# A hybrid Conformer and mLSTM backbone on one core: the scheduler's default state against a timeline of every engine

## The chip, the core and the metric

One Trainium2 chip, one of its cores. A core has five engines with a queue of instructions each: TensorE (PE, matrix products into PSUM), VectorE (DVE) and ScalarE (ACT) for elementwise work, GpSimd (POOL), and SyncE (SP), which here only issues DMAs from HBM to SBUF. Each engine takes its queue in order, and an instruction waits on semaphores for those of other engines. The metric is the device time in microseconds (us) of one launch: the median of several runs.

## The reference

Two layers over 256 latent and 256 context tokens of width 1024, in float32. Layer 0 mixes tokens with a Conformer convolution, layer 1 with a bidirectional chunkwise mLSTM of 4 heads; after each comes a squared-ReLU MLP of width 4096. Every part is modulated by adaLN (shift, scale and gate from a condition vector) and followed by a layer norm:

```python
def adaln(cvec, w, b):
    return jnp.split(jax.nn.silu(cvec) @ w + b, 6, axis=-1)

def modulate(x, shift, scale):
    return x * (1 + scale) + shift

def conformer_conv(u, rows, w_pw1, b_pw1, w_dw, b_dw, ln_g, ln_b, w_pw2, b_pw2):
    a = u @ w_pw1 + b_pw1
    a = a[..., :CONV_DIM] * jax.nn.sigmoid(a[..., CONV_DIM:])
    ...
    a = jax.nn.silu(layer_norm(a + b_dw, ln_g, ln_b))
    return a @ w_pw2 + b_pw2
```

The sub-layer is `x <- LN(ALPHA*x + gate * F(modulate(x)))`; the output is the latent stream, 256 x 1024.

## The kernel before

**Products.** A float32 product is made of three products of a faster type. `split` (L150, L151) makes of a tile a rounded high half (ACT casts `wh`) and the rest as a low half (DVE subtracts, `wl`); `mm3` (L181, L184, L185) adds hi·hi, hi·lo and lo·hi in PSUM. `mm3t` (L212 to L214) does the same with the operands exchanged, `mm_any` (L196, L197) with a right side that holds both halves. Weights come in tiles `raw` of 1 MB, of which there are three buffers, all loaded on SP (`raw_load`, L144); a tile `raw` is split into two pairs `wh`, `wl` of 1024 columns, of which there are four each. The PSUM tags are mm (3 banks), ln (2), fl (1) and cv (2).

**The start** (L607 to L664). The first modulation and the first pointwise product of the Conformer run in eight stages f = 0 to 7, each over 128 of the 1024 features. `start0(f)` loads three things on SP: `raw` with the adaLN weights (1 MB), `x` (256 KB, L622) and `F` with pointwise weights (256 KB, L624); then `ada_mm` (L343) makes the modulation of these features on PE, and DVE copies it (L630). `start1(f)` splits `F` into wh, wl, folds the modulation on PE (L351), makes shift and scale on DVE (L637, L638), and `affine_split` makes the modulated tile `u` with its halves: ACT the high half (L600), DVE the product again (L601) and the low half by subtraction (L603). `start2` multiplies: 4 output tiles by 3 matmuls. They are written so that the L343 of stage f+1 goes ahead of the products of stage f:

```python
    for f in range(DT):
        start2(f, (0,))
        if f + 1 < DT:
            start1(f + 1)
        start2(f, (1, 2, 3))
        if f + 2 < DT:
            start0(f + 2)
    pin[0] = False
    later = tc.high_priority(-100)
    later.__enter__()
```

**Behind it** lies a block of lower priority (L669 to L741) that builds tables of cosines for the convolution by DFT: DVE steps L696 to L713 on a tile `tab`, loads of `bdw` and of two tiles `L` with the taps, and `taps` (L739), two matmuls per half. Then the rest of the pointwise product with weights `pw1`, the transform, and the later layers follow. `ada_mm` also makes the later modulations, of which `fl_136_759` is the next.

**What sets the order.** The code is written in Python, and the framework's scheduler turns it into one queue per engine. It may take an instruction ahead of others where no data and no buffer forbid it, and places it by priority and by its own picture of when engines and data are ready. The code binds it in three ways: `tc.issue_after(i)` puts what is issued in it behind instruction i, `tc.keep_in_program_order` pins a matmul among others that are pinned (only while `pin[0]` holds, in the start), and `tc.high_priority(-100)` makes a block less urgent. Nothing pins the loads, ACT or DVE in the start beyond that. The scheduler also gives out the buffers in that order, so which earlier use a load waits for depends on it, and it spreads the semaphores of the DMAs of SP and ACT over eight: from the ninth DMA on an issue waits for the landing of an earlier one.

## Time and profile before

| | us |
|---|---|
| median of 3 runs | 1661.2 |
| lowest, highest | 1659.6, 1662.05 |
| span of the profiled execution | 1658.8 |
| PE busy in it | 1647.3 |
| DVE busy | 1042.7 |
| ACT busy | 730.4 |

The page gives for each engine its busy time and share of the span, then the chain of work that ended last, followed back from the last instruction, in shares of the span by engine. The view of waits lists, for an engine, line and releaser, the idle time in total, how often, and the longest. A row of the timeline has the start, the length, the engine, the line, the operation, out<-in, partitions and elements, how many instructions it joins, and in brackets the idle time before it with what ended it. "SPq" is an issue of a DMA on SP, which says nothing yet of its landing; the first reader's wait shows that. A matmul of 512 columns starts about 0.23 us behind the one before, though its row says 0.39: they overlap. The table over stretches gives for a window its length, then busy time and count of PE, PEld (weight loads), DVE, ACT and POOL, the clock granted to TensorE, the busy share of the DMA engines and GB/s.

### The profile page before, as it was taken

The page shows a single profiled execution, that of the slowest core. Times are in us where ns is not written, and L with a number is a line of the kernel's source. Part 1 is how long each engine was busy: PE and PEld are TensorE (multiplying, and loading weights), DVE is VectorE, ACT ScalarE, POOL GpSimd, SP SyncE. Part 2 cuts the span into 40 slices and gives each one's busy share as a digit, 9 for nine tenths or more (in the row PEclk, how much of TensorE's full clock was granted, in tenths as well). Part 3 has the DMA queues.
Part 4 walks back from the last instruction along what each step waited for, and adds up shares of the span by engine and source line. Part 5 has one row for each costly group of instructions (what it writes and reads, how often), then busy time and mean ns, then how long its engine had stood idle before and what let it go on. Part 6 is the DMA issues. An engine that isn't in the chain of part 4 may idle for free.

```text
span 1658.8 us, 22681 instructions
## 1 busy us (share of the span) xinstructions
PE 1647.3 (99%) x8824; PEld 1357.0 (82%) x8824; DVE 1042.7 (63%) x1875; ACT 730.4 (44%) x1174; POOL 14.3 (1%) x64
## 2 busy tenths in 40 slices
PE   9999999999999999999999999999999999999998
PEld 7665998888888998877787899888878888878887
DVE  6564895666535776762254753563489776776677
ACT  4313572232324475652133533442478654555453
POOL 0000000000000000000000000000000000000001
PEclk9999999999999999999999999999999999999999
DMA  9666223434424066557774852554466655675552
GB/s 359 229 213 239 96 71 116 163 123 147 137 102 153 1 225 204 184 194 272 282 255 145 301 179 80 178 190 151 147 227 219 212 211 202 242 283 186 178 186 93
DMA packets 80411, 305.80 MB, mean 184 GB/s; under 512 B 11854, under 2 KB 30066, under 8 KB 50352
## 3 DMA queue, kind: packets, MB, share of 16 engines
q1 hardware_dynamic: 57840, 288.06, 49.5%
q10 hardware_dynamic: 22464, 16.30, 3.0%
q8 instruction: 69, 1.13, 0.3%
q14 instruction: 38, 0.31, 0.1%
HBM read 286.47 MB, written 17.86 MB: 183 GB/s over the span
## 4 chain that ended last, share of the span: by engine, by line
PE 93%; DVE 4%; DMA 1%; ACT 1%; issue 1%; SPq 0%; DVEq 0%; ACTq 0%
PE mm L181 17%; PE mm L184 17%; PE mm L185 17%; PE mm L196 7%; PE mm L197 4%; PE mm L212 3%; PE mm L214 3%; PE mm L213 3%; PE cv L212 2%; PE fl L343 1%; PE cv L214 1%; PE cv L213 1%; DVE wl L151 1%; PE ln L181 1%; PE cv L878 1%; PE ln L184 1%
## 5 line engine op out<-in xcount | busy, mean ns | idle before, releaser
L151 DVE TENSOR_TENSOR wl<-raw,wh 128x1024 fp32r<-128x1024 f32 x344 | 418.5, 1221 | 248.1 <-ACT wh L150 246.5
L150 ACT CAST wh<-raw 128x1024 fp32r<-128x1024 f32 x344 | 358.6, 1051 | 463.3 <-PE mm L184 245.1
L184 PE MATMUL mm<-u,wh 128*128 128x512 f32 (+1 forms) x808 | 292.2, 362 | 0.2 <-DVE u L603 0.2
L181 PE MATMUL mm<-u,wh 128*128 128x512 f32 (+1 forms) x680 | 244.1, 360 | 0.0
L185 PE MATMUL mm<-u,wl 128*128 128x512 f32 (+1 forms) x680 | 241.5, 356 | 0.0
L184 PEld LDWEIGHTS mm<-u,wh 128*128 128x128 f32 x808 | 153.0, 189 | 23.3 <-issue 1.0
L181 PEld LDWEIGHTS mm<-u,wh 128*128 128x128 f32 x680 | 128.8, 190 | 24.9 <-issue 6.3
L185 PEld LDWEIGHTS mm<-u,wl 128*128 128x128 f32 x680 | 128.8, 190 | 17.9
L212 PE MATMUL mm<-wh,xl 128*128 128x512 f32 x256 | 101.2, 395 | 0.9 <-ACT wh L150 0.8
L181 PE MATMUL mm<-xm,wh 128*128 128x512 f32 x256 | 101.0, 395 | 0.0
L213 PE MATMUL mm<-wh,xl 128*128 128x512 f32 x256 | 100.0, 391 | 0.0
L185 PE MATMUL mm<-xm,wl 128*128 128x512 f32 x256 | 99.7, 389 | 0.0
L214 PE MATMUL mm<-wl,xl 128*128 128x512 f32 x256 | 99.4, 392 | 0.1
L181 PE MATMUL mm<-hid,wh 128*128 128x512 f32 (+1 forms) x256 | 93.3, 364 | 0.0
L185 PE MATMUL mm<-hid,wl 128*128 128x512 f32 (+1 forms) x256 | 92.8, 363 | 0.0
L184 PE MATMUL mm<-hid,wh 128*128 128x512 f32 (+1 forms) x256 | 92.8, 363 | 0.0
L196 PE MATMUL mm<-x,wh 128*128 128x512 f32 x232 | 81.1, 398 | 0.0
L184 PE MATMUL mm<-qq,wh 128*128 128x272 f32 x256 | 73.9, 289 | 0.0
L181 PE MATMUL mm<-qq,wh 128*128 128x272 f32 x256 | 73.5, 288 | 0.0
L185 PE MATMUL mm<-qq,wl 128*128 128x272 f32 x256 | 73.5, 288 | 0.0
L196 PE MATMUL mm<-u,wh 128*128 128x512 f32 x192 | 68.6, 399 | 0.0
L1120 DVE SCALAR_TENSOR_TENSOR x<-mm,ada,x 128x256 f32<-128x256 f32 x64 | 28.5, 479 | 62.4 <-PE mm L185 62.4
(537 smaller groups left out, 3245.2 us busy)
## 6 DMA issues: line engine op xcount, KB each, us to landing
raw<-w SPq DMA_DIRECT2D x64, 1024.0 KB, 4.8
raw<-wo SPq DMA_DIRECT2D x32, 1024.0 KB, 5.3
raw<-ada_w SPq DMA_DIRECT2D x22, 1024.0 KB, 7.3
ar<-ada_w SPq DMA_DIRECT2D x80, 256.0 KB, 4.1
raw<-wv SPq DMA_DIRECT2D x16, 1024.0 KB, 7.3
raw<-wqT SPq DMA_DIRECT2D x16, 1024.0 KB, 5.6
raw<-wq SPq DMA_DIRECT2D x16, 1024.0 KB, 6.2
raw<-wk SPq DMA_DIRECT2D x16, 1024.0 KB, 4.8
```

Source lines behind the costliest of these rows:

```text
L150: c = nc.scalar.copy(hi, src)
L151: lastsub[0] = nc.vector.tensor_tensor(lo, src, hi.bitcast(F32), op=ALU.subtract).ins
L181: a = nc.tensor.matmul(ps, wh, xh, start=start, stop=False)
L184: nc.tensor.matmul(ps, wh, xl, start=False, stop=False)
L185: lastmm[0] = nc.tensor.matmul(ps, wl, xh, start=False, stop=stop).ins
L196: todo = [lambda s_, e_: nc.tensor.matmul(ps, wh, r[0], start=s_, stop=e_), lambda s_, e_: nc.tensor.matmul(ps[:, :n], wl, r[0][:, :n], st ...
L197: lambda s_, e_: nc.tensor.matmul(ps[:, :n], wl, r[0][:, :n], start=s_, stop=e_)]
L212: nc.tensor.matmul(ps, xh, wh, start=start, stop=False)
L213: nc.tensor.matmul(ps, xl, wh, start=False, stop=False)
L214: nc.tensor.matmul(ps, xh, wl, start=False, stop=stop)
L343: a = mark_unit[0] = nc.tensor.matmul(ps[32 * j:32 * j + 32], cs[:, kt, 14 - 2 * v:46 - 2 * v], blocks[kt], start=first and kt < 4, stop=l ...
L1120: nc.vector.scalar_tensor_tensor(res[m][:, sl_], p_, g[:, m:m + 1], res[m][:, sl_], op0=ALU.mult, op1=ALU.add)
```

## The change

One argument where the scheduler is set up:

```diff
-    with _tile.TileContext(nc) as tc:
+    with _tile.TileContext(nc, schedule_with_timeline_sim=True) as tc:
         hybrid_kernel(tc, *args, o)
```

The scheduler now keeps a simulated timeline of every engine while it orders the program, and places by that. `hybrid_kernel` is the same text: the same loads, matmuls and elementwise steps, and two loads of ACT's function tables fewer (26 for 28). What differs is the order on each engine, and with it the buffers and the waits. PE has 2526 lines of difference among some 8150, DVE 1857, ACT 1067, SP 246, POOL 30. PE's order in the first seven stages of the start is the same. Three places, in which the numbers of tiles are those of the program (`F_19_171` is stage 1's F, `F_30_217` stage 2's, `F_85_447` stage 7's; `u_91_472` and `u_92_473` are the halves of stage 7's u):

On SP, in the start, from stage 1's x on (`raw_29_214` is stage 2's raw, `x_28_213` to `x_83_443` are the x of stages 2 to 7):

```order
 L622 DMA x_17_167<-xT 128x512
-L624 DMA F_19_171<-pw1a 128x512
 L144 DMA raw_29_214<-ada0_w 128x2048
 L622 DMA x_28_213<-xT 128x512
+L622 DMA x_39_259<-xT 128x512
+L622 DMA x_50_305<-xT 128x512
+L622 DMA x_61_351<-xT 128x512
+L622 DMA x_72_397<-xT 128x512
+L622 DMA x_83_443<-xT 128x512
+L624 DMA F_19_171<-pw1a 128x512
```

Stage 1's F, before the third load behind stage 1's raw, is now the ninth: all x and the next raw go first. Right behind it on SP, in the same way, up to stage 2's F (`raw_40_260` and `raw_51_306` are the raw of stages 3 and 4, `bdw` and the two `L` belong to the block of tables):

```order
+L144 DMA raw_40_260<-ada0_w 128x2048
+L728 DMA bdw_570<-wdw_d 128x1024
+L733 DMA L_99_574<-wdw_d 31x512
+L733 DMA L_100_575<-wdw_d 31x512
+L144 DMA raw_51_306<-ada0_w 128x2048
 L624 DMA F_30_217<-pw1a 128x512
```

Two raw of later stages and the loads of the tables now go ahead of it.

Before stage 7, first SP again (`raw_115_614` and `raw_125_683` are weights pw1 for the products behind the start, `raw_134_755` adaLN weights for `fl_136_759`):

```order
 L624 DMA F_74_401<-pw1a 128x512
-L144 DMA raw_84_444<-ada0_w 128x2048
-L622 DMA x_83_443<-xT 128x512
-L624 DMA F_85_447<-pw1a 128x512
-L144 DMA raw_101_579<-wg_d 128x256
 L144 DMA raw_115_614<-pw1 128x2048
 L144 DMA raw_125_683<-pw1 128x2048
+L624 DMA F_85_447<-pw1a 128x512
 L144 DMA raw_134_755<-ada_w 128x2048
```

Stage 7's F now stands behind the two raw of pw1. On DVE there, from the stage's scale to the low half of its u, before:

```order
L638 TENSOR_SCALAR sc1p_109<-ln_90_467,vecs_72 128x2
L699 TENSOR_SCALAR tab_524<-F_94_509,pc_510 128x128
L601 TENSOR_SCALAR S_93_474<-x_83_443,sc1p_109,sh1p_110 128x256 x2
L700 TENSOR_SCALAR tab_524<-F_94_509,pc_510 128x128
L701 TENSOR_SCALAR tab_524<-tab_524 128x63
L603 TENSOR_TENSOR u_92_473<-S_93_474,u_91_472 128x512
```

and now:

```order
L638 TENSOR_SCALAR sc1p_109<-ln_90_467,vecs_72 128x2
L706 TENSOR_TENSOR tab_524<-tab_524,F_95_531 128x384
L151 TENSOR_TENSOR wl_117_617<-raw_115_614,wh_116_616 128x1024
L601 TENSOR_SCALAR S_93_474<-x_83_443,sc1p_109,sh1p_110 128x256 x2
L707 SCALAR_TENSOR_TENSOR F_95_531<-tab_524 128x384
L151 TENSOR_TENSOR wl_120_647<-raw_115_614,wh_119_646 128x1024
L151 TENSOR_TENSOR wl_127_686<-raw_125_683,wh_126_685 128x1024
L708 TENSOR_SCALAR tab_524<-F_95_531 128x384
L603 TENSOR_TENSOR u_92_473<-S_93_474,u_91_472 128x512
```

Three of the four small steps are done earlier; three subtractions of whole weight tiles and three wider steps of the tables stand between now. ACT has the three casts that belong to them ahead of its half of `u`.

On PE, between stage 6 and stage 7 (`cv_4_108` is stage 6's last product, `mm_1_105` stage 7's first; `fl_136_759` stood about 120 matmuls later, behind the products with pw1):

```order
 L184 MATMUL cv_4_108<-u_81_427,wh_77_417 128x512
 L185 MATMUL cv_4_108<-u_80_426,wl_78_418 128x512
+L343 MATMUL fl_136_759<-raw_134_755,cs_91 32x512 x4
 L181 MATMUL mm_1_105<-u_91_472,wh_88_463 128x512
 L184 MATMUL mm_1_105<-u_92_473,wh_88_463 128x512
```

The first half of the next modulation, four matmuls with their raw, has come ahead of stage 7.

## The prediction

> **What bounds the kernel now.** First the page: busy times, then the chain of work that ended last.
>
> ```profile
> PE 1647.3 (99%) x8824; PEld 1357.0 (82%) x8824; DVE 1042.7 (63%) x1875; ACT 730.4 (44%) x1174; POOL 14.3 (1%) x64
> ...
> PE 93%; DVE 4%; DMA 1%; ACT 1%; issue 1%; SPq 0%; DVEq 0%; ACTq 0%
> ```
>
> TensorE is busy in 99% of a span of 1658.8 us, and 93% of the chain is its own. So I ask first how much an order could win, by the view of waits, on PE:
>
> ```profile
> PE cv L175 <- DVE ones L129: 1.1, 1, 1.1
> PE mm L212 <- ACT wh L150: 0.8, 1, 0.8
> PE ln L739 <- DVE tab L713: 0.5, 1, 0.5
> PE fl L343 <- DMA raw<-ada_w: 0.3, 1, 0.3
> PE cv L878 <- DVE F L867: 0.3, 1, 0.3
> PE mm L184 <- DVE u L603: 0.2, 1, 0.2
> PE ln L549 <- DVE ln L537: 0.2, 1, 0.2
> ```
>
> All of PE's waits together are 3.4 us, 1.1 of them the program's first. The one other loss is the clock: full in all 40 slices of the page, but by a table over stretches
>
> ```profile
> 41.90:63.60 21.70, 21.21 (x81) 16.20 (x82) 17.98 (x34) 8.66 (x11) 1.99 (x8) 0.93 0.72 238
> ```
>
> it was 0.93 over these 21.7 us, which is 1.5 us lost. With the same matmuls an order can win at most some 4 us (3.4 - 1.1 + 1.5). It can lose wherever a producer with little to spare is put later, and the start is such a place: there each of eight stages needs three loads that have just come.
>
> **The loads of stages 1 and 2.** Before, SP issues for each stage raw (1 MB of 1024 KB), x and F (256 KB each). Now five further x stand ahead of stage 1's F, and raw, bdw, two L and another raw ahead of stage 2's. PE's order in stages 0 to 6 is pinned and stays. What a place in the queue costs is read from ACT's timeline, where the cast of stages 1 to 4 starts when its F lands, and from two issues on SP:
>
> ```profile
> 11.44 0.62 ACT L150 CAST wh<-F 128x512 fp32r<-128x512 f32 x1 [0.97 <-DMA F<-pw1a]
> 15.18 0.62 ACT L150 CAST wh<-F 128x512 fp32r<-128x512 f32 x1 [0.73 <-DMA F<-pw1a]
> 20.28 0.62 ACT L150 CAST wh<-F 128x512 fp32r<-128x512 f32 x1 [1.76 <-DMA F<-pw1a]
> 24.03 0.62 ACT L150 CAST wh<-F 128x512 fp32r<-128x512 f32 x1 [1.02 <-DMA F<-pw1a]
> ```
>
> ```profile
> 3.84 0.66 SPq L624 DMA_DIRECT2D F<-pw1a  x1
> ...
> 33.42 4.73 SPq L144 DMA_DIRECT2D raw<-pw  x2
> ```
>
> The F issued at 3.84 lands at 15.18: 11.3 us for 256 KB, so it waits for what was issued ahead of it. From 11.44 to 24.03 three stages of 1.5 MB came in 12.6 us, 0.36 MB per us; the best of them took 3.74 us, 0.40. I take 0.38. Now PE's rows at the places concerned, and the end of DVE's work for a stage:
>
> ```profile
> 10.29 1.07 PE L343 MATMUL fl<-raw,cs 128*32 128x256 f32 x16 [0.29 <-DMA raw<-ada_w]
> ...
> 16.03 0.40 PE L184 MATMUL mm<-u,wh 128*128 128x512 f32 x1
> ...
> 20.43 0.40 PE L184 MATMUL mm<-u,wh 128*128 128x512 f32 x1
> ...
> 32.28 1.07 PE L343 MATMUL fl<-raw,cs 128*32 128x256 f32 x16
> ...
> 36.69 1.07 PE L343 MATMUL fl<-raw,cs 128*32 128x256 f32 x16
> ...
> 41.92 0.50 PE L184 MATMUL mm<-u,wh 128*128 128x512 f32 x1 [0.23 <-DVE u L603]
> ```
>
> ```profile
> 23.05 0.69 DVE L603 TENSOR_TENSOR u<-S,u 128x512 fp32r<-128x512 f32 x1 [0.39 <-ACT u L600]
> ```
>
> Stage 1's raw has landed by 10.2 (PE waited for it until 10.29). Behind it now come x, raw, six x and F: 0.25 + 1 + 1.5 + 0.25 = 3.0 MB, or 7.9 us: F at 18.1 (17.7 to 18.5 by the two rates) instead of 11.4. From a landed F to the low half of u it is 23.74 - 20.28 = 3.5 us, so stage 1's second matmul goes from 16.03 to 21.6: 5.5 us late. Behind that F stand 1 + 0.5 + 0.12 + 1 + 0.25 = 2.87 MB, 7.6 us: stage 2's F at 25.7, its u at 29.2, against 20.43: **8.7 us late** (7.9 to 9.5). The 5.5 are contained in it. Stages 3 to 6 have one raw and one F each to wait for, 3.3 us against 4.4 us of PE work per stage, and their x are there: nothing more.
>
> **Stage 7.** Three edits meet. On SP its F stands behind two raw of pw1. The first row of SP above shows what these wait for: the issue at 33.42 follows the end of PE's L343 of 32.28 (33.35), the second, at 37.8, that of 36.69 (37.76): a slot of the three raw buffers. The second raw now takes the slot that the L343 of 32.28 frees, so it is issued at 33.35 + 8.7 = 42.0 and F at 42.4. How long that takes is on the page:
>
> ```profile
> raw<-w SPq DMA_DIRECT2D x64, 1024.0 KB, 4.8
> ...
> ar<-ada_w SPq DMA_DIRECT2D x80, 256.0 KB, 4.1
> ```
>
> raw lands at 46.8, F 0.25 / 0.38 = 0.7 later: 47.5 (46.5 if it needs only 4.1; 50 if the raw ahead still fills the queue). Then DVE. Between the stage's scales and the subtraction L603 that makes u stand, instead of four small steps, L706 to L708 of the tables and three subtractions of whole weight tiles, and ACT has three casts ahead of its half of u. Their lengths in DVE's timeline:
>
> ```profile
> 39.07 0.68 DVE L151 TENSOR_TENSOR wl<-F,wh 128x512 fp32r<-128x512 f32 x1
> ...
> 40.12 0.73 DVE L601 TENSOR_SCALAR S<-x,sc1p,sh1p 128x256 f32<-128x256 f32 x2
> ...
> 41.17 0.69 DVE L603 TENSOR_TENSOR u<-S,u 128x512 fp32r<-128x512 f32 x1
> ...
> 42.57 0.56 DVE L706 TENSOR_TENSOR tab<-tab,F 128x384 f32<-128x384 f32 x1
> ...
> 44.18 0.55 DVE L707 SCALAR_TENSOR_TENSOR F<-tab 128x384 f32<-128x384 f32 x1
> 44.76 0.36 DVE L708 TENSOR_SCALAR tab<-F 128x384 f32<-128x384 f32 x1
> ...
> 47.58 3.46 DVE L151 TENSOR_TENSOR wl<-raw,wh 128x1024 fp32r<-128x1024 f32 x3
> ```
>
> Cast of F 0.62, then 0.68 + 0.56 + 3.46 + 0.73 + 0.55 + 0.36 + 0.69 = 7.0 on DVE: 7.6 us, all needed in a row. u is ready at 55.1, against PE's 41.92, where it had nothing to spare (it waited 0.23): PE is **13.2 us late** (12 to 16), the 8.7 included. Third, four matmuls of L343 for the next modulation, 32 us early on PE, stand ahead of stage 7. Their raw waits for the slot that the L343 of 36.69 frees, is issued at 46.5 and lands at 51.3 to 53; with 1.0 us of work they end by 54, inside the wait that is there anyway. Where they stood they are missing:
>
> ```profile
> 73.24 1.06 PE L343 MATMUL fl<-raw,cs 128*32 128x512 f32 x8
> ```
>
> which gives 1.0 us back. Without DVE's part of the wait they would cost that instead. L739's first two matmuls stand ten matmuls earlier than before, but PE is 12 us late there, and DVE reaches the table's last step L713 some 6 us after stage 7's u, at 61, while PE comes at about 69: its 0.5 us wait is gone. Start: 13.2 - 1.0 - 0.5 = 11.7.
>
> **The clock.** The lost 1.5 us may go with L739's wait, or come again behind the new gaps. I take nothing, with -1.5 and +3 as ends (the same dip gone, or twice more). The Trainium skill, "TensorE: Matmul & The Clock Gate", section "HAM oscillation — how this bites in real kernels", warns of idle gaps over about 3.4 us, behind which the matmuls run at half clock. No gap of this trace is longer than 1.1 us, and its dip came without one, so no run here shows it yet; it speaks against this change.
>
> **The rest of the program.** Most of it moves by a few us on engines that have them to spare. Three places have not:
>
> ```profile
> 1201.58 1.21 DVE L151 TENSOR_TENSOR wl<-raw,wh 128x1024 fp32r<-128x1024 f32 x1
> ...
> 1274.76 1.27 DVE L1673 SCALAR_TENSOR_TENSOR og<-ln,vecs,raw 128x256 f32<-128x256 f32 x3 [1.83 <-PE ln L1669]
> ...
> 1281.21 1.28 DVE L1607 TENSOR_TENSOR og<-mm,bo 128x512 f32<-128x512 f32 x2
> ...
> 1471.03 0.28 DVE L1821 TENSOR_TENSOR x<-S,x 128x128 fp32r<-128x128 f32 x1
> ```
>
> ```profile
> 1202.84 0.50 PE L214 MATMUL mm<-wl,xl 128*128 128x512 f32 x1
> ...
> 1282.26 0.39 PE L212 MATMUL mm<-wh,xl 128*128 128x512 f32 x1
> ...
> 1471.46 0.50 PE L196 MATMUL mm<-x,wh 128*128 128x512 f32 x1
> ```
>
> At 1202.84 PE starts as wl is done (1202.79); now small steps of the gates (L1425 to L1437) stand ahead of that subtraction, 1.4 us more: 0 to 1.4, and for want of a nearer row I take the middle, 0.7. At 1282.26 PE takes the PSUM bank that the first L1607 frees at 1281.9; now the chain of decays (S, es, pw) and a weight split stand ahead of it, by rows 6.4 us more; PE's matmul has moved 0.9 back, which leaves 1.3 to spare: 5.1 at most. DVE idled 1.83 us just there, which the moved work can fill: 3.3. I take 3, from 0 to 5.1. At 1471.46 x is ready 0.15 us ahead; now six more of L1816's scalings of the same tile and one more L1821 come first, 2.1 us at this row's 0.3: 0 to 2, I take 1. Together 4.7 (0 to 8.5).
>
> **The sum.** 11.7 + 0 + 4.7 = 16.4 us on a span of 1658.8: 1675.2. The median of the runs shown is 1661.2, 2.4 above the span, which holds what lies around it and the spread of runs and isn't touched: **1678**. Bounds: 12 - 1.5 - 1.5 + 0 = 9 gives 1670; 16 - 1.5 + 3 + 8.5 = 26 gives 1687.
>
> **The rivals.** *Small loads pass big ones; no slower.* If a 256 KB load needs only the page's 4.1 us whatever is queued, stage 1's F, issued behind an x that waits for the landing at 10.2, is there at 14.7 and its u at 18.2: 2.2 us late, stage 2 not at all. The last F then is issued at 33.35 + 2.2 + 0.4 = 36.0, lands at 40.1, and u is ready at 47.7: 5.8 late. Less 1.0, 0.5 and the dip's 1.5, and with nothing in the later places, that is 2.8: 1664, within 0.2%, which is 3.3 us and about what a measurement of this kernel can tell. It decides if stage 1's cast starts before 15.2. Against it stand the 11.3 us of the F issued at 3.84. The Trainium skill, "DMA: Bandwidth & Descriptors", section "Two DMAs through the same engine are not ordered", says that nothing orders transfers across the 16 engines; by that rule this could be; the casts above, 3.7 to 5.1 us apart, show landings that go by bytes. Chance 0.08.
>
> *The later places cost all they can.* 11.7 + 8.5 = 20.2: 1681. For it: DVE is the bound there in stretches; against it: it had idle time to give. Chance 0.17.
>
> *The clock halves behind the long gaps.* Stage 1's half speed would be hidden by stage 2's wait (6 us), stage 7's not: 1.5 once or twice on top of the forecast, 1680 to 1681. Chance 0.15.
>
> *Something in the new order wins that I don't see*, up to the 4 us: below 1658. Chance 0.05. That the change does nothing is excluded by the order of the instructions.
>
> **How the numbers follow.** The forecast has 0.55. Slower by over 0.2% are it and the second and third rival: 0.87. The first rival gives the 0.08 of no change, the last the 0.05 of faster. The range, the bounds of the sum with some room toward the first rival, leaves out the last and the first: 1666 to 1689.
>
> **What would show it.** In the profile after: ACT's casts of F at 18.1 and 25.7; PE waits for DVE u L603 or ACT u L600 of 5 and 3 us before stages 1 and 2 and, with L343's raw, some 5 to 6 ahead of stage 7; the second matmul of stage 7 near 55; L739's wait gone; PE waits at L212 near 1295 and at L196 near 1487. It is wrong if the casts come with F at 11 to 15, or if the start costs 12 and the time is below 1666, which would mean that the rest won.

## The result, and the profile after

The changed kernel takes 1731.1 us (median of 4 runs, 1727.55 to 1733.48) against 1661.0 us (4 runs, 1659.6 to 1662.05): a ratio of 1.043 (95% interval 1.0415 to 1.044), 70 us slower. The forecast was 17 us slower, in a range up to 1689: the sign was right, the size wrong by a factor of four.

The profiled execution, the slowest of the four, has a span of 1731.6 us, 72.8 more than before. The page, three lines of it:

```profile
span 1731.6 us, 22705 instructions
...
PE 1677.9 (97%) x8824; PEld 1369.0 (79%) x8824; DVE 1039.8 (60%) x1875; ACT 728.1 (42%) x1172; POOL 13.7 (1%) x64
...
PEclk8899999999999999999999999999998999999999
```

PE ran the same 8824 matmuls and was busy 30.6 us longer; the other 42 us of the loss are idle time. DVE and ACT did the same work as before. A digit of the row PEclk is the granted clock of a slice of 43.3 us in tenths: it is under 0.9 in the first two slices, to 87 us, and in the one from 1299 to 1342 us. Shorter stretches at half clock don't show in it. The view of waits on PE, whose sum was 3.4 us before and is 45.0 now:

```profile
PE mm L181 <- ACT u L600: 10.6, 2, 5.8
PE mm L212 <- DVE og L1607: 7.5, 2, 4.7
PE fl L343 <- DMA raw<-ada_w: 4.5, 3, 3.7
PE mm L212 <- ACT og L150: 3.8, 1, 3.8
PE ln L1669 <- ACT og L1661: 2.4, 2, 2.2
PE mm L196 <- DVE x L1821: 2.0, 1, 2.0
PE mm L212 <- ACT wh L150: 1.7, 1, 1.7
PE mm L184 <- DVE u L594: 1.7, 4, 0.7
PE mm L184 <- DVE u L603: 1.6, 1, 1.6
```

Of the 45.0 us, 18.8 lie in the start, up to 75 us of before's time, and 23.0 behind 1192; the other 3.2 lie between 75 and 300 us, L594 among them. The table over stretches shows where the clock was low, and one stretch without loss:

```profile
0.00:68.00 68.00, 50.19 (x299) 35.29 (x300) 33.62 (x104) 20.35 (x37) 3.11 (x16) 0.85 0.71 266
...
300.00:1160.00 860.00, 859.95 (x4584) 722.29 (x4583) 485.72 (x787) 334.16 (x533) 2.40 (x33) 1.00 0.51 175
...
1320.00:1345.00 25.00, 15.05 (x53) 11.05 (x52) 19.12 (x50) 18.53 (x31) 0.00 (x0) 0.73 0.39 143
```

If the same matmul is looked up in both traces, PE is some 26 us late at 50 us of before's time, 34 at 250, still 33 at 1100, 43 at 1200 and 72 from 1500 on. So the loss lies at the start, in the stretch up to 300 us, around 1100 to 1200 us, and behind that. The start in the new trace, first ACT's casts of F for stages 1, 2, 3 and 7, then PE's waits:

```profile
18.39 0.62 ACT L150 CAST wh<-F 128x512 fp32r<-128x512 f32 x1 [7.30 <-DMA F<-pw1a]
...
31.32 0.62 ACT L150 CAST wh<-F 128x512 fp32r<-128x512 f32 x1 [10.21 <-DMA F<-pw1a]
...
34.93 0.62 ACT L150 CAST wh<-F 128x512 fp32r<-128x512 f32 x1 [0.87 <-DMA F<-pw1a]
...
58.65 0.62 ACT L150 CAST wh<-F 128x512 fp32r<-128x512 f32 x1 [4.74 <-DMA F<-pw1a]
```

```profile
21.17 0.79 PE L181 MATMUL mm<-u,wh 128*128 128x512 f32 x1 [4.76 <-ACT u L600]
...
34.10 0.80 PE L181 MATMUL mm<-u,wh 128*128 128x512 f32 x1 [5.84 <-ACT u L600]
...
61.92 1.93 PE L343 MATMUL fl<-raw,cs 128*32 128x512 f32 x8 [3.70 <-DMA raw<-ada_w]
...
66.16 0.80 PE L184 MATMUL mm<-u,wh 128*128 128x512 f32 x1 [1.58 <-DVE u L603]
```

Stage 1's F came as forecast (18.1). Stage 2's came 5.6 us later than forecast, and stage 7's second matmul, forecast at 55.1, starts at 66.16. The rows say 0.8 for a matmul that takes 0.4 to 0.5 before: half clock.

### The profile page after: what moved, and what is told of

Read it like the earlier page. It is cut to its first block, busy times and chain, and to the rows that moved or that the text cites. A ratio compares the mean times of both kernels' runs of the same rounds, so it can differ in the third digit from the quotient of the medians.

```text
span 1731.6 us, 22705 instructions
## 1 busy us (share of the span) xinstructions
PE 1677.9 (97%) x8824; PEld 1369.0 (79%) x8824; DVE 1039.8 (60%) x1875; ACT 728.1 (42%) x1172; POOL 13.7 (1%) x64
## 4 chain that ended last, share of the span: by engine, by line
PE 89%; DVE 5%; DMA 3%; ACT 1%; issue 1%; SPq 0%; DVEq 0%; ACTq 0%
PE mm L181 17%; PE mm L184 16%; PE mm L185 16%; PE mm L196 7%; PE mm L197 3%; PE mm L212 3%; PE mm L214 3%; PE mm L213 3%; DMA F<-pw1a 2%; PE cv L213 1%; PE cv L212 1%; PE cv L214 1%; PE cv L1256 1%; PE cv L878 1%; PE ln L184 1%
## 5 line engine op out<-in xcount | busy, mean ns | idle before, releaser
L181 PEld LDWEIGHTS mm<-u,wh 128*128 128x128 f32 x680 | 127.8, 191 | 39.2 <-ACT u L600 13.2
L185 PEld LDWEIGHTS mm<-u,wl 128*128 128x128 f32 x680 | 129.8, 191 | 18.8 <-issue 0.8
L212 PE MATMUL mm<-wh,xl 128*128 128x512 f32 x256 | 103.1, 403 | 10.7 <-DVE og L1607 7.5
L213 PE MATMUL mm<-wh,xl 128*128 128x512 f32 x256 | 102.3, 400 | 0.5 <-DVE xl L151 0.5
L212 PEld LDWEIGHTS mm<-wh,xl 128*128 128x128 f32 x256 | 49.4, 193 | 21.8 <-DVE og L1607 7.7
```

What stands on the lines that cost most here:

```text
L181: a = nc.tensor.matmul(ps, wh, xh, start=start, stop=False)
L185: lastmm[0] = nc.tensor.matmul(ps, wl, xh, start=False, stop=stop).ins
L212: nc.tensor.matmul(ps, xh, wh, start=start, stop=False)
L213: nc.tensor.matmul(ps, xl, wh, start=False, stop=False)
```

## The experiments

In all runs the program is the same and only the order on the engines is set, except where the text says more: the order is written out, engine by engine, as numbers of instructions, and laid as an edge without a semaphore between neighbours; data and buffers are still waited for as the framework finds it.

```diff
         hybrid_kernel(tc, *args, o)
+        _queue(tc, nc, _mybir)
```

The diffs below show what the table of numbers says. The kernel before, run along with each, took 1659.4 to 1660.4 us; differences in us are against that.

### The start alone, and its loads alone

```diff
-every engine, up to 75.5 us: order of before
+every engine, up to 75.5 us: order of after
 every engine, behind it: order of before
```

> The program before, with the order of the program after on every engine up to where the kernel before stood at 75.5 us (start and products with pw1), and its own order from there on. Theory (the losses add up, the start has its own): the loss that the trace after shows at that place, 25 to 27 us, alone: 1687 us, with stage 7's second matmul near 66 as in after. Rival (the start's delay is partly paid back by engines that wait less later): under 1680.

Measured: 1685.43 us (ratio 1.0154, 1.0139 to 1.017), 25.2 us more. The casts of F stand at 18.00, 31.04 and 58.27. So the start costs 25 us by itself, twice the 11.7 of the forecast, and nothing behind it takes the loss back.

Then only SP's first 40 loads in after's order, the rest as before:

```diff
-SP, first 40 loads: order of before
+SP, first 40 loads: order of after
 PE, DVE, ACT, POOL: order of before
```

> The order before on PE, DVE, ACT and POOL; on SP the first 40 loads in the order of after. Theory (what delays the start is the order of the loads, and the clock behind the gaps): stage 2's F lands at 31, stage 7's F at about 58, PE 20 to 24 us late at stage 7, 1683 us. Rival (the recorded prediction: loads cost 8.7 us and the rest is DVE's order before stage 7): F of stage 2 at 26, PE 9 to 11 us late, 1671 us.

Measured: 1681.66 us (1.013, 1.0115 to 1.0145), 21.4 us more. Casts of F at 18.86, 30.80 and 59.67. PE's waits, one line:

```profile
PE mm L181 <- ACT u L600: 15.1, 3, 6.1
```

The loads alone cost 21 of the 25 us. The orders of PE, DVE and ACT together, of which the forecast made DVE's and ACT's responsible for much of stage 7, add the other 4.

### The taps behind the F that they held up

Stage 2's F came at 31.3 and not at 25.7. Ahead of it on SP stand, besides two raw and bdw, the two `L` of 31 partitions, 62 KB each. In after's order they were moved:

```diff
 L728 DMA bdw_570<-wdw_d 128x1024
-L733 DMA L_99_574<-wdw_d 31x512
-L733 DMA L_100_575<-wdw_d 31x512
 ...
 L144 DMA raw_134_755<-ada_w 128x2048
+L733 DMA L_99_574<-wdw_d 31x512
+L733 DMA L_100_575<-wdw_d 31x512
```

> The order after on all engines, except that SP issues the two loads of L (31 partitions, 62 KB each) behind the raw of the next modulation instead of ahead of stage 2's F. Theory (a load over 31 partitions is carried by a few of the 16 DMA engines, and what stands behind it waits for those): stage 2's F lands at about 26 instead of 31.3, PE's 5.8 us wait there falls to under 2, 1724 to 1727 us. Rival (loads queue by bytes, 0.12 MB is 0.3 us): F at 31.0, 1731 us.

Measured: 1723.62 us (1.0385, 1.0368 to 1.0403), 7.5 less than after. ACT's cast of stage 2's F, and PE's first matmul of stage 2:

```profile
25.34 0.62 ACT L150 CAST wh<-F 128x512 fp32r<-128x512 f32 x1 [5.07 <-DMA F<-pw1a]
```

```profile
28.12 0.51 PE L181 MATMUL mm<-u,wh 128*128 128x512 f32 x1 [1.09 <-ACT u L600]
```

With the taps out of the way F lands where the forecast put it, 6.0 us earlier, and the wait of 5.84 falls to 1.09. Stage 1's F came 0.8 us earlier in this run too (17.55 for 18.39), so 5.1 of the 6.0 lie between the two F. 0.12 MB counted as bytes is 0.3 us; in front of F it was worth some 5. In the run with the loads alone, where F landed at 30.80, the 16 DMA engines were nearly idle while it was still awaited (the last two numbers are their busy share and GB/s):

```profile
29.00:30.00 1.00, 0.56 (x12) 0.08 (x4) 0.00 (x0) 0.00 (x0) 0.00 (x0) 1.00 0.09 35
```

A share of 0.09 is that of one or two engines of 16. This fits a load that few engines carry, though it does not show which load they were on.

The 7.5 us are a difference to runs of another session; taken against the kernel before run beside each, they are 6.7.

### The start with PE kept at work

The matmuls behind the gaps of the start run at half clock. Does that cost time of its own? To the kernel with the loads alone (PE idle for 6.1, 4.0 and 4.9 us) come products of the tile of ones into an unused PSUM bank, which change no result:

```diff
     for f in range(DT):
+        if f in (1, 2, 7):
+            idle(spare, {1: 20, 2: 24, 7: 20}[f])
         start2(f, (0,))
```

> Before's order with the first 40 loads of SP as after (1681.7 us, PE idle 6.1, 4.0 and 4.9 us ahead of stages 1, 2 and 7, half-clock windows of 10.2, 6.8 and 6.8 us behind), and 20, 24 and 20 further products of the tile of ones (two passes of 0.14 us each, 0.27 us) into an unused PSUM bank ahead of the first product of stages 1, 2 and 7. They change no result; they keep PE at work while it waits, for 5.4, 6.5 and 5.4 us. Theory: the clock halves because PE sits idle, and what it costs comes on top of the wait. Stage 1's slow matmuls only shorten stage 2's wait, since its F comes by the queue; stage 2's 6.8 us and stage 7's 6.8 us of half clock cost some 3.4 and 2 us. Then 1681.7 - 5 = 1676.7 (1675.5 to 1678.5), the granted clock of the span 0.998 or more, and the casts of F where they were. Rival: the half clock costs nothing of its own, since the next wait takes it up: 1680.5 to 1683. Second rival: the window has other causes than the idle time and stays: same time, clock 0.991.

Measured: 1680.88 us (1.0125, 1.011 to 1.014), 0.8 less than with the loads alone, which is inside the intervals; against the kernel before run beside each, the two cost 21.5 and 21.4 us. The stretch 0 to 68 us, first with the loads alone, then filled:

```profile
0.00:68.00 68.00, 51.36 (x302) 37.06 (x303) 30.19 (x97) 22.54 (x39) 3.04 (x16) 0.82 0.67 250
```

```profile
0.00:68.00 68.00, 61.37 (x436) 48.61 (x437) 30.70 (x98) 23.88 (x41) 3.03 (x16) 0.97 0.67 251
```

The clock of the stretch went from 0.82 to 0.97 (3.41 us of half clock are left, at 35.06) and the time stayed. The filled kernel waits for stage 7's u until 62.56 us, the other until 62.45: up to there the first rival holds, since what PE loses to the clock between two loads it would otherwise lose waiting for the next. Behind stage 7 no load ends the wait. There, matmul by matmul, the filled kernel is 1.35 us ahead at 70 us, and then gives part back, because it now comes too early for the table:

```profile
79.69 1.98 PE L741 MATMUL ln<-L,tab 31*128 31x512 f32 x4 [0.43 <-DVE tab L715]
```

(L741 is L739 of the other kernels.) At 90 us it is 0.75 ahead. My theory that some 5 us come on top fell. What the half clock costs in the full order of after, with the other engines in their new order too, was not tried.

### The stretch from 75 to 300 us

```diff
 every engine, up to 75.5 us: order of before
-every engine, 75.5 to 300 us: order of before
+every engine, 75.5 to 300 us: order of after
 every engine, behind it: order of before
```

> Before's order up to 75.5 us, after's order from there to 300 us, before's order behind. Theory: the change's loss is a sum of places; start alone 25.2, end alone 27.9 and the gates of L1256 11.0 leave 70.1 - 64.1 = 6 for the rest, most of it in this stretch: 1660.3 + 6 = 1666 (1664.5 to 1669), with L853's groups of two bursts each costing some 2 us. Rival: what after lost there came from its late start (loads and buffers shifted by 25 us), so the stretch alone costs under 2 us: 1660 to 1662.

Measured: 1668.69 us (1.0057, 1.004 to 1.0074), 9.3 us more, the upper edge of what was expected; the span is 7.6 above before's. PE's waits grew by some 3 us (1.7 at L594, 0.8 for E at L1096, 0.7 at L1012), at no clock loss. Two us more are in the products L853, whose rows of the timeline say 64*128: they use 64 of the 128 rows of the array. Before and after:

```profile
92.68 0.69 PE L853 MATMUL ln<-A,tab 64*128 64x512 f32 x1
92.69 0.69 PE L853 MATMUL mm<-A,tab 64*128 64x512 f32 x1
```

```profile
104.28 1.98 PE L853 MATMUL ln<-A,tab 64*128 64x512 f32 x4
...
119.60 1.12 PE L853 MATMUL mm<-A,tab 64*128 64x512 f32 x2
...
128.18 1.12 PE L853 MATMUL mm<-A,tab 64*128 64x512 f32 x2
```

Before, a matmul of `ln` and one of `mm` start 0.01 us apart: they run side by side, and two such pairs take 1.1 us. After, each tile's matmuls stand alone, 4.2 us in all for 2.2. The rest of the 9 us is not taken apart.

### The gates put together again

The same at L1256, a product of gates in four column tiles of 32, each matmul of which shows as two rows. Before, the eight rows of a group mostly stand together; after, more groups are pulled apart by other matmuls. One group before, and four of the bursts after:

```profile
1116.72 1.41 PE L1256 MATMUL cv<-raw,wgq 128*32 128x512 f32 x8
```

```profile
1150.11 1.06 PE L1256 MATMUL cv<-raw,wgq 128*32 128x512 f32 x6
...
1154.55 1.04 PE L1256 MATMUL cv<-raw,wgq 128*32 128x512 f32 x2
...
1165.49 1.05 PE L1256 MATMUL cv<-raw,wgq 128*32 128x512 f32 x2
...
1176.66 1.05 PE L1256 MATMUL cv<-raw,wgq 128*32 128x512 f32 x4
```

A burst takes 1.05 us whether it has 2 rows, 4 or 6, and the others of 8 rows take 1.06 to 1.15. Before has 9 bursts for its eight groups, after 16. In after's order, on PE alone, each of the five groups that stand in 13 bursts was put where its last matmul stood; one of these five stands in two bursts before, too. One of the five:

```diff
-L1256 MATMUL cv_1134_6667<-raw_1653_10069,wgq_583 32x512
 ...
-L1256 MATMUL cv_1134_6667<-raw_1653_10069,wgq_583 32x512 x2
 ...
-L1256 MATMUL cv_1134_6667<-raw_1653_10069,wgq_583 32x512
+L1256 MATMUL cv_1134_6667<-raw_1653_10069,wgq_583 32x512 x4
```

> The order after on all engines, except that the four matmuls of L1256 of each group stand together on PE again, at the place of the last of them (five groups had been pulled apart into 13 bursts). Theory (four matmuls of 32 columns run side by side in the array, a burst takes 1.05 us whether it holds two rows or eight): 8 bursts fewer at 1.1 us each, 9 us, 1722 us. Rival (the growth of PE's busy time there is switching between operand types or missing operands): 1729 to 1731 us.

Measured: 1720.07 us (1.0366, 1.0351 to 1.0382), 11.0 less than after (10.3 against the kernel before run beside each). PE's busy time fell by 10.8 us, to 1667.1: the loss is PE's own busy time, and no view of waits shows it. Not all of the 11.0 is what the change pulled apart. Matmul by matmul the run is 0.8 us ahead of after in front of these groups and 10.1 behind the last, so 9.3 us are theirs, and 1.4 of these lie at the group that is in two bursts before as well. That leaves 7.9. The rest came around 1325 us, where half clock lasted 10.24 us in this run's trace and 13.65 in after's.

### The end alone, and its loads alone

```diff
-every engine, behind 1192 us: order of before
+every engine, behind 1192 us: order of after
```

> The order before on every engine up to where the kernel before stood at 1192 us (the end of the gate products), and the order after from there on. Theory (losses add up): the loss that the trace after builds up from there, 72.5 - 43 = 29 to 31 us, alone: 1690 us, with PE's waits at L212 for L1607 and for the casts of og, and L196 for L1821. Rival (these waits come from the shift of the start and of the loads against each other): under 1680.

Measured: 1688.27 us (1.0172, 1.0158 to 1.0186), 27.9 us more. PE's waits are after's own of that region:

```profile
PE mm L212 <- DVE og L1607: 7.5, 2, 4.7
PE mm L212 <- ACT og L150: 3.8, 1, 3.8
PE ln L1669 <- ACT og L1661: 2.4, 2, 2.2
PE mm L196 <- DVE x L1821: 1.9, 1, 1.9
```

Then SP alone in after's order behind 1192 us:

```diff
-SP, behind 1192 us: order of before
+SP, behind 1192 us: order of after
```

> The order before, except that SP issues its loads from 1192 us on in the order of after. Theory (the end is lost in the order of DVE and ACT, its loads only follow the buffers that these free): 1660 to 1664 us. Rival (as in the start, the order of the loads is the cause): 1670 us or more.

Measured: 1669.57 us (1.006, 1.0047 to 1.0074), 9.2 us more. The theory that loads only follow fell: alone they cost a third of what the end costs. But the profiled run, the slowest of the four at 1672.41 us, has a wait of 2.8 us from 1246.7 on for a weight, which after's full order does not have; so the 9.2 us are not the loads' share in the full order:

```profile
PE mm L212 <- ACT wh L150: 4.5, 2, 2.8
```

How the loss of the full order divides among PE, DVE, ACT and the loads was not tried engine by engine. Two single moves were.

### Two casts, and then the decays, out of the way of L1607

Ahead of PE's wait of 4.7 us for L1607, ACT casts a late weight tile before it does L1656 and L1661, which the sum L1607 stands behind. To the end alone:

```diff
-ACT: L150 CAST wh_1895, wh_1897 ahead of L1656 and L1661
-DVE: L151 wl_1896, wl_1898 ahead of L1657 and L1658
+ACT: L1656, L1661, then the two casts
+DVE: L1657, L1658, then the two subtractions
```

> As the end alone, but two casts of a weight tile of wo on ACT (wh_1895, wh_1897) stand behind the two L1661 and their subtractions on DVE behind L1658, instead of ahead of the decays and of the group norm's steps. In the trace after ACT waits 4.3 us there for the landing of that raw. Theory (a cast that waits for its load holds up the group norm behind it on ACT, and with it the L1607 for whose PSUM bank PE waits): PE's 4.7 us wait for L1607 shrinks by 4 or more and the half clock behind it with it: 6 to 10 us less than the end alone, some 1682 us. Rival (the recorded prediction: DVE has too much to do ahead of L1607, S, es, pw): within 2 us of the end alone.

Measured: 1693.0 us (1.0196, 1.0182 to 1.021), 4.7 slower than the end alone. The theory fell. PE needs that very cast ahead of all the rest, and waits for it and for L1607 longer than before:

```profile
PE mm L212 <- DVE og L1607: 8.3, 2, 5.5
PE mm L212 <- ACT wh L150: 6.1, 1, 6.1
```

Next the steps that the forecast had named, the decays (S, es, pw) on DVE and their exponentials and casts on ACT. PE reads them over 200 matmuls later:

```diff
-DVE: 18 steps S_1891 to S_1909, es_1877, pw ahead of L1607 (og_1876)
-ACT: 13 exponentials and casts of S_1891 to S_1961 ahead of L1608 (og_1876)
+the same behind them
```

> The order of the end alone (before's order up to 1192 us, after's behind: 1688.3 us), but on DVE 18 steps of the decays of the next but one group (S_1891 to S_1909, es_1877 and their pw) stand behind the second L1607 (og_1876) instead of ahead of the L1673s, and on ACT 13 (their exponentials and casts, with the two of S_1961) behind the L1608s instead of ahead of the L1661s. PE needs them over 200 matmuls later. Theory: the sums L1607 come late because these steps stand ahead of the chain L1661, L1669, L1673, L1607 on both engines: 5.9 us of DVE and 5 us of ACT with a switch of the function table. L1607 comes 3 to 5 us earlier, PE's wait of 4.7 us for it falls to 0 to 1.7, and with the half clock behind it that is 3 to 6 us: 1682.3 to 1685.3. Rival: the chain starts when the late weight tile wo (raw_1894) has been cast, as the run with the casts later suggests, and the wait moves: 1687 to 1690.

Measured: 1688.52 us (1.0174, 1.0159 to 1.0189), no change, as the rival had it and not the theory. Yet L1607 moved as expected: DVE starts it at 1289.78 us instead of 1294.40. PE's rows around it, with the end alone, and then with the decays later:

```profile
1286.18 0.44 PE L1669 MATMUL ln<-ident,og 128*128 128x128 f32 x2 [2.16 <-ACT og L1661]
...
1295.14 0.79 PE L212 MATMUL mm<-wh,xl 128*128 128x512 f32 x1 [4.68 <-DVE og L1607]
```

```profile
1290.52 0.80 PE L212 MATMUL mm<-wh,xl 128*128 128x512 f32 x1 [2.91 <-DVE og L1607]
...
1301.39 0.50 PE L212 MATMUL mm<-wh,xl 128*128 128x512 f32 x1 [3.01 <-ACT wh L150]
```

PE goes on 4.6 us earlier, and 11 us later waits 3.0 us for a cast that the moved steps now hold up (it starts at 1300.30 for 1297.67); 20 us on it is no earlier than without the move. The cause named by the forecast is real, but its gain is given back at once. Neither move touched what stands ahead of both, ACT's wait for the load of the late weight tile, here with the end alone:

```profile
1279.01 2.00 ACT L150 CAST wh<-raw 128x1024 fp32r<-128x1024 f32 x2 [4.20 <-DMA raw<-wo]
```

After has the same wait (4.27, at 1322.02), and with the decays later it is 4.27 still. At the same casts ACT waited 1.52 us before. Whether the end is lost by this late tile, or by too much work on ACT and DVE around it, no run shows.

### A version that beats both

Before's order was kept, with after's only from 500 to 640 us, where after had gained a fraction of a us, and the two matmuls of L739 that waited 0.46 us were put nine matmuls later on PE:

```diff
-L739 MATMUL ln_98_675<-L_99_574,tab 128x512
-L739 MATMUL ln_98_678<-L_99_574,tab 128x512
 ...
+L739 MATMUL ln_98_675<-L_99_574,tab 128x512
+L739 MATMUL ln_98_678<-L_99_574,tab 128x512
```

> The order before, with the order of after only from 500 to 640 us, where the trace after gained 0.8 us, and with L739's first two matmuls nine matmuls later than before. Theory (its 0.5 us wait goes, and the half clock behind it, 1.7 us): 3 us less, 1657.3 us. Rival (the clock drops there for the small matmuls themselves, wait or no wait): 1.2 us less, 1659.2 us, not to be told from no change.

Measured: 1657.94 us (11 runs) against 1660.36 (15 runs), a ratio of 0.9986 (0.9977 to 0.9995), so of the 4 us that the forecast allowed an order to win, 2.4 are there (0.8 to 3.8 by the interval). The two edits were not tried apart. The wait at L739 and the clock's dip at 60 us are gone, but that the one ends the other isn't shown: the runs of the end alone, of 75 to 300 us and of the decays later have before's order there, the same wait of 0.44 to 0.47 us, and no dip either.

## Why the prediction was wrong, point by point

**What bounds the kernel.** That PE is the bound, that an order can win at most some 4 us and that it loses where producers have little to spare was right. The start alone, the stretch to 300 us, the gates and the end alone add up to 25.2 + 9.3 + 11.0 + 27.9 = 73.4 us, against 70.1 measured: the loss is a sum of places. With the 7.9 us of the gates that the change itself pulled apart, it is 70.3. The forecast had priced 11.7 for the first, 4.7 for the last, and nothing for the two between.

**Stage 1 behind 3.0 MB: right.** F at 18.1, measured 18.39; u 5.5 us late, measured 5.9 (21.89 for 16.03, the next matmul behind the 21.17 of the row above).

**Stage 2 behind 2.87 MB: the step that failed first.** F was put at 25.7 by "1 + 0.5 + 0.12 + 1 + 0.25" MB at 0.38 MB per us. The 0.12 is not worth its bytes: F came at 31.32, and at 25.34 with the two loads of 31 partitions moved. The Trainium skill, "DMA: Bandwidth & Descriptors", section "Why a DMA increments its semaphore by 16 and not by 1", says that a load uses the largest number of engines up to 16 that divides the slowest dimension on both of its sides; of the numbers up to 16 only 1 divides 31. An estimate by that rule and the measured rate: 0.124 MB through one of 16 engines at 0.38 / 16 MB per us is 5.2 us, and the run showed 5.1 behind stage 1's F (6.0 in all); it agrees, though the traces here don't show the single engines.

**Stage 7: the place right, two terms mis-sized.** From the cast of F at 58.65 to the end of u at 66.1 it took 7.5 us, against 7.6 forecast, and the four matmuls of `fl_136_759` with their raw lay within that wait. But F was put at 47.5, issued at 42.4. The issues on SP, of the two raw of pw1 and of F:

```profile
48.78 1.99 SPq L144 DMA_DIRECT2D raw<-pw  x2
50.86 0.43 SPq L624 DMA_DIRECT2D F<-pw1a  x1
```

F was issued at 50.86, 8.5 us later than forecast; 5.6 of these are stage 2's further delay, which as I read it passes through PE's L343 to the slots of raw. Another 2.6 came in stage 2 itself, whose matmuls ran at half clock: from its second matmul to the next L343 it was 5.6 us (34.83 to 40.45) and not 3.05. F then took 7.8 us to its cast, behind two raw, and not 5.1. PE reached its second matmul 24 us late, not 13.2. Most of that is the loads: with before's order on DVE and ACT, where u follows F by 3.5 us, it was 21 us late already. The chain on DVE, 7.5 us for 3.5, is 4.0 longer, but its F came 1.0 earlier than in that run, which makes the other 3.

**The wait at L739** went, as forecast.

**The clock.** Taken as nothing, with 3 us as the end. Half-clock stretches came behind each gap of 2.8 us or more, as the third rival said, and filling the gaps of the start was worth under 1 us. The rival's sizes were near: stage 1's was hidden by the next load, stage 7's brought 1.35 us for its 1.5, of which the wait at L739 took part back. So the number for the clock held in that run, by luck more than by reason: it was taken from before's trace, which has no such gap to show, and in after's own order the 2.6 us of stage 2 above were not priced at all. The Trainium skill's warning, "TensorE: Matmul & The Clock Gate", section "HAM oscillation — how this bites in real kernels", of half clock behind gaps over about 3.4 us is borne out behind 3.7 to 5.84 us; but half clock came behind 2.83 us too, and the time it counts for it was not lost where a load ended the next wait. What the stretches at the end cost, behind gaps of 2.2 to 4.7 us, no run took apart.

**The rest of the program: the step that failed most.** "Most of it moves by a few us on engines that have them to spare" was said of 2526 lines of difference on PE, of which three places were looked up. Two errors stand in it. The first is to count PE's matmuls as the same work in any order: those of 32 columns or of 64 rows cost less side by side, and some 10 us went where the order pulled them apart (7.9 of the 11.0 measured at L1256, 2.0 read from L853's rows). The second is to price the end by the spare time of single instructions. At the places named the waits were near: 4.7 us at L1607, given 3 of a bound of 5.1; 0.4 at the first, given 0.7; 2.0 at L1821, given 1. Not seen were a second wait for L1607 (2.8, at 1399 us), L1661 (2.4), the cast of og (3.8), and that a wait that is removed there comes back elsewhere, as the two moves showed.

**The rivals.** That small loads pass big ones fell: stage 1's cast came at 18.39, not before 15.2. One of the reasons given against it was misread: the F issued at 3.84 is stage 1's and lands at 11.44, so it took 7.6 us, not 11.3. That is still more than 4.1, and no term of the sum hangs on it. That the later places cost all they can was on the right side, and far too small.

**Still open:** how the 28 us of the end divide between the loads, DVE, ACT and PE's own order, and what of them the clock and the late weight tile make; what the half clock of stage 2 cost in after; and 4 of the 9 us between 75 and 300 us.

## What to carry to other kernels

When an order is changed all over, look up every wait of a tuned order that is just met, and every group of small matmuls that runs side by side; a mean over thousands of lines of difference says nothing of either. Price a queue of loads by how many partitions each load has, not by bytes alone. And before counting a half clock or a removed wait as time, ask what ends the next wait: filled gaps and an earlier L1607 both changed the profile and not the time.

## What the runs showed of the hardware

Half clock comes in whole stretches. The granted clock of before's dip at 60 us, and of two stretches of after, behind gaps of 5.84 and 2.83 us:

```profile
60.42:63.83 3.41, 3.41 (x9) 2.63 (x9) 1.23 (x1) 1.54 (x2) 0.00 (x0) 0.50 0.41 100
```

```profile
33.31:40.14 6.83, 6.04 (x16) 4.61 (x16) 3.88 (x10) 2.96 (x6) 0.00 (x0) 0.50 0.04 16
...
1398.64:1405.47 6.83, 5.99 (x14) 4.73 (x15) 2.61 (x4) 3.89 (x5) 0.00 (x0) 0.50 0.55 192
```

In after they last 3.41, 6.83, 10.24 or 13.65 us, once to four times 3.41 (but for one that the end of the run cuts), and begin 2 to 5 us behind the start of the idle time. Behind a single gap, 2.83 us was enough; 2.17 us was, at 1329, with a gap of 1.71 six us ahead of it; behind 1.95 us, at 1543, there was no half clock. Before's dip came behind 0.46 us of idle time and the matmuls of 31 rows at L739, but not in three runs with the same order and wait there. And a group of matmuls on 32 columns takes 1.05 us for 2, 4 or 6 rows alike.
